# Bidirectional retention on one Trainium2 core: value and gate projections by seven block products in heads 1 to 7, the output summed in DRAM, gate and output weights placed anew

## The chip, the core and the metric

The kernel runs on one core of a Trainium2 chip, as one program written with a tile framework that places buffers, sets semaphores and orders the instructions of each engine. The engines are TensorE (PE, matrix products; PEld is its loading of weights), VectorE (DVE), ScalarE (ACT), GpSimd (POOL) and SyncE (SP, which here only issues loads). The metric is the device time of one execution in microseconds (us).

## The reference, cut to what matters

Two layers over 512 latent tokens and 256 context tokens of width 1024, all in float32. Layer 1 mixes tokens by retention; the change is in this mixer alone.

```python
q, k, v, g = jnp.split(h_lat @ w_in, splits, axis=-1)      # 8 heads: q, k 128 wide, v, g 256 wide
q = apply_rope(q); k = apply_rope(k * dk ** -0.5)
kc, vc = jnp.split(h_ctx @ w_in[:, ...], ...)              # context: k and v only
for d in range(2):                                         # forward and backward in time
    s_ctx = retention_final_state(kc, vc, log_decay[d])    # state carried in from the context
    o[d] = retention_chunked(q, k, v, log_decay[d], s_ctx) # decayed q.k scores times v, plus decayed q times state
on = group_norm_per_head(o[0] + o[1]) * gn_g
y_lat = (silu(g) * on) @ w_out                             # sum over the 8 heads
x = x + g1 * rmsnorm(y_lat)
```

## The kernel before, in words

Every product is made in three TensorE passes on float32 operands cut in two: `mm3` (L94 to L96) multiplies high by high, high by low and low by high. `split` makes the two halves: ACT copies the source to `hi` (L68), DVE subtracts to get `lo` (L69). A weight block is 128x1024 float32 (512 KB). `unit` loads it by SP (L54) into one of three "raw" buffers, and splits it into a weight slot. The slots go round; there are three (`w0` to `w2`) and in the retention three more (`phase("retp", 3)`). The raw buffers are shared with `ar`, the rows of the adaLN projection, a background job (`self.bg()`) that DVE sums (L214).

The order of instructions on each engine is fixed when the program is built, and each engine takes its list in order; semaphores make it wait for the others. In the retention, tiles of PSUM come from three pools of 4 (A), 2 (B) and 2 (C) banks.

Head 0 is written out for itself, among the work that ends layer 0. Each of the heads 1 to 7 does, in this order on PE:

- `rk`: the latent k projection (24 matmuls with 512 columns); meanwhile DVE does the end of the previous head's `norm`;
- `rt` and `rq`: `gated` transposes the previous head's gated output (8 transposes), and the q projection follows (24);
- `wr`: `out_group` multiplies the previous head's output by its two weight blocks `rwo`, and DVE adds each of the eight results into the sum `yr` in SBUF (L494);
- `kn`: transposes of k, decayed on ACT and DVE into `kd`;
- `rn` for v: three pairs of 128 tokens (context, latent, latent), each 48 matmuls with 256 columns, with the scores `rs` between them;
- `stc`, `stl`: `states` multiplies `kd` by v for the context and one latent chunk; a chain over ACT and DVE (`st`, `sc`, `cm`, `st`; L68, L1013, L1015, L69) makes the chunk states;
- `rn` for the gate: two pairs, 96 matmuls, each pair through SiLU on ACT (L1040);
- `ro` (`within`, chunk 0), two `rx` (`across`, from the states; DVE adds them into `of`, L1078), `rkc` (the next head's context k), `ro` (chunk 1), two `rx`, and `norm` (DVE L1094 to L1112 with a short piece on POOL, L1098 and L1101).

After head 7, `out_last` multiplies the outputs of heads 6 and 7 and passes the rows on to the second half of the layer.

Of the kernel before, what the change touches and what calls it, by code (L numbers as in the profile page):

```python
# [16 lines left out]
P = 128  # L17
D = 1024
# [22 lines left out]
class Trunk:  # L41
# [871 lines left out]
    def retention(self, y, final):  # L913
        S, V, T, G, a = self.S, self.V, self.T, self.G, self.a
        KS = float(np.float32(P) ** np.float32(-0.5))
        with ExitStack() as ctx:
            rp = self.phase(ctx, "retp", 3)
# [11 lines left out]
            qk = lambda h, o, n: self.unit(a["ret_qk"][(o + h) * P : (o + h + 1) * P], f"rw{n}{h}")  # L929
            vg = lambda h, o, n: [  # L930
                w8(self.unit(a["ret_vg"][(o + h * 2 + i) * P : (o + h * 2 + i + 1) * P], f"rw{n}{h}{i}"))
                for i in range(2)
            ]
# [92 lines left out]
            def nat(h, w, tp, dst):  # L1026
                ps = self.ps(f"rn{h}{tp}", "A", (P, 2, 256))
                for i in range(2):
                    hc = self.hcols(2 * tp + i)
                    for kk in range(KD):  # L1030
                        wk = w[kk // 4]
                        self.mm3(
                            ps[:, i, :], hc(kk), (wk[0][:, kk % 4, :], wk[1][:, kk % 4, :]), kk == 0, kk == KD - 1
                        )
                t = slice(2 * tp, 2 * tp + 2)
# [10 lines left out]
            def score(h, c):  # L1046
# [9 lines left out]
                s2 = d[c] = [rp.tile([P, 2, 256], F32R, name=f"sd{i}{h}{c}", tag=f"sd{i}", bufs=2) for i in range(2)]  # L1056
# [30 lines left out]
            def norm(h):  # L1087
# [14 lines left out]
                for t in range(4):  # L1102
                    on = rp.tile([P, 256], F32, name=f"on{h}{t}", tag="on", bufs=2)
# [11 lines left out]
            def gated(h):  # L1115
                d = hd[h]
                if h == 7:
                    gt = [x.rearrange("p (f c) -> p f c", f=2) for x in self.slot("gt7")]
                else:
                    gt = [rp.tile([P, 2, 512], F32R, name=f"gt{i}{h}", tag=f"gt{i}", bufs=1) for i in range(2)]  # L1120
# [16 lines left out]
            def w_out(h):  # L1137
                return [self.unit(a["ret_out"][(2 * h + f) * P : (2 * h + f + 1) * P], f"rwo{h}{f}") for f in range(2)]

            toks = (0, 1, 2, 3)  # L1140

            for h in range(8):
                vg_tiles(h)
                if h == 0:
                    wk = qk(h, 8, "k")
                    self.need(2)
                    k_ctx(h, wk)
                    wv = vg(h, 0, "v")
                    nat(h, wv, 2, "v")
                    self.need(0)  # L1150
                    wq = qk(h, 0, "q")
                    wg = vg(h, 16, "g")
# [3 lines left out]
                    for half in range(2):  # L1156
# [6 lines left out]
                        for n, f in enumerate(steps):  # L1163
# [6 lines left out]
                            if half and n == 2:  # L1170
                                k_nat(h)
                                score(h, 0)
                                score(h, 1)
                                states(h)
                    self.bg(4)
                else:
                    psk = self.ps(f"rk{h}", "A")
                    self.proj_t(psk, wk, 0)
                    k_lat(h, psk)
                    wq = qk(h, 0, "q")  # L1180
                    psq = self.ps(f"rq{h}", "A")
                    decay(h)
                    f = gated(h - 1)
                    self.proj_t(psq, wq, 0)
                    q_lat(h, psq)
                    self.bg()
                    if h < 7:
                        self.out_group(f, w_out(h - 1), y, toks, h == 1, None, f"r{h - 1}")
                    k_nat(h)
                    self.bg()  # L1190
                    wv = vg(h, 0, "v")
                    for tp in (2, 0, 1):
                        nat(h, wv, tp, "v")
                        if tp < 2:
                            score(h, tp)
                    self.bg()
                    wg = vg(h, 16, "g")
                    states(h)
                    for tp in range(2):
                        nat(h, wg, tp, "g")  # L1200
# [10 lines left out]
                if h < 7:  # L1211
                    k_ctx(h + 1, wk)
# [520 lines left out]
```

## Time and profile before

| | |
|---|---|
| median of 3 runs | 1902.22 us (1896.47 to 1906.23) |
| the profiled execution | 1893.99 us, of which the span from first to last instruction is 1892.2 us |
| mean granted TensorE clock in it | 0.983 |
| PE busy | 1800.1 us, 95% of the span, 10928 instructions |
| DVE, ACT, POOL busy | 1402.8, 1029.2 and 325.8 us |
| moved by DMA | 250.32 MB, mean 132 GB/s |

The clock is a share of full speed: 1.00 is full, 0.50 half. In the profile's lists of groups, a row names the line of the kernel, the engine, the operation, the tiles written and read, and behind the bar the busy time and the mean duration. "Idle" in brackets, or behind a second bar, is the time in which the engine stood still just ahead of the row, and the arrow names what it waited for. In a list by stretches (A:B, in us from the start) each row gives the length, then the busy time of PE, PEld, DVE, ACT and POOL with the instructions in brackets, the granted clock, the share of the DMA engines and GB/s. The answer for one tile gives its instructions with least, median and longest duration in ns, and the starts of the first and the last.

### The profile page before, as it was taken

What the parts mean: (1) busy time and instruction counts of PE and PEld (TensorE: products, weight loads), DVE (VectorE), ACT (ScalarE), POOL (GpSimd) and SP (SyncE); (2) the same over time, 40 slices, a digit from 0 to 9 for tenths busy, and PEclk for the clock granted to TensorE, in tenths of its full rate; (3) what the DMA queues carried; (4) which work ended last, traced back from release to release, by engine and by line L of the source; (5) the groups of instructions that cost most, each with busy time, mean ns of one, the idle gap of its engine ahead of it and who ended that gap; (6) DMA issues with size and microseconds to landing.
All of it is one profiled execution on the core that took longest, in us unless ns stands there. A gap on an engine that the chain in (4) does not pass through costs nothing. (4 is left out here: it accounts for less than half of the span.)

```text
span 1892.2 us, 28751 instructions
## 1 busy us (share of the span) xinstructions
PE 1800.1 (95%) x10928; PEld 1591.7 (84%) x10928; DVE 1402.8 (74%) x2352; ACT 1029.2 (54%) x1857; POOL 325.8 (17%) x446
## 2 busy tenths in 40 slices
PE   7998989979999999999989999999999989999998
PEld 4886867669889899998879889988989779889996
DVE  4844788679877778777877666675665689989877
ACT  6533545666555555555565434434444377666763
POOL 1102122130122222222121010011011100222221
PEclk9999999999999999999989999999999989999999
DMA  7333332132577877776744313322421225878772
GB/s 290 115 100 106 93 101 79 57 136 76 175 176 156 184 158 167 145 169 135 232 146 131 119 52 112 112 95 62 134 66 48 100 81 148 212 188 195 178 162 99
DMA packets 83823, 250.32 MB, mean 132 GB/s; under 512 B 10578, under 2 KB 12114, under 8 KB 83684
## 3 DMA queue, kind: packets, MB, share of 16 engines
q1 hardware_dynamic: 58436, 200.72, 32.8%
q0 software_dynamic: 25248, 47.75, 15.2%
q8 instruction: 86, 1.41, 0.3%
q14 instruction: 53, 0.43, 0.1%
HBM read 191.81 MB, written 39.85 MB: 122 GB/s over the span
## 5 line engine op out<-in xcount | busy, mean ns | idle before, releaser
L214 DVE SCALAR_TENSOR_TENSOR acc<-ar,cs,acc 128x512 f32<-128x512 f32 x256 | 189.5, 758 | 35.5 <-DMA ar<-in_adaw 19.7
L1463 POOL DMA_DIRECT2D yf<-yp x64 | 55.9, 873 | 260.2 <-ACT yp L1459 229.2
L1314 ACT ACTIVATE cv<-pre,cw 128x770 f32<-128x770 f32 (+1 forms) x88 | 80.9, 923 | 27.2 <-DVE pre L1307 25.9
L1315 DVE SCALAR_TENSOR_TENSOR cv<-pre,cw,cv 128x769 f32<-128x769 f32 (+1 forms) x88 | 77.2, 880 | 7.2 <-ACT cv L1314 7.2
L1459 ACT COPY yp<-wf 128x512 f32<-128x512 f32 x118 | 67.9, 577 | 18.1 <-PE wf L96 18.0
L1318 DVE SCALAR_TENSOR_TENSOR cv<-pre,cw,cv 128x769 f32<-128x769 f32 (+1 forms) x88 | 77.2, 881 | 0.7
L1302 ACT ACTIVATE pre<-px 128x256 f32<-128x256 f32 (+2 forms) x160 | 54.3, 367 | 41.8 <-PE px L93 33.6
L1098 POOL TENSOR_SCALAR rrr<-rmv 128x2 f32<-128x2 f32 x16 | 3.1, 193 | 363.2 <-DVE rmv L1095 363.2
L1463 POOL DMA_DIRECT2D yd<-ypg x48 | 42.1, 903 | 132.1 <-ACT ypg L1459 130.6
L1463 POOL DMA_DIRECT2D yd<-yp x48 | 42.6, 902 | 126.7 <-ACT yp L1459 126.6
L68 ACT ACTIVATE g<-cv 128x770 fp32r<-128x770 f32 (+1 forms) x44 | 32.5, 738 | 32.6 <-DVE cv L1322 32.4
L93 PE MATMUL px<-hs,wd 128*128 128x384 f32 x240 | 45.4, 337 | 0.0
L93 PEld LDWEIGHTS px<-hs,wd 128*128 128x128 f32 x240 | 42.3, 188 | 1.9 <-DVE pre L1307 0.4
L1307 DVE TENSOR_TENSOR pre<-pre,pz 128x256 f32<-128x256 f32 (+1 forms) x60 | 20.8, 371 | 29.2 <-PE pz L96 29.1
L69 DVE TENSOR_TENSOR g<-cv,g 128x770 fp32r<-128x770 f32 (+1 forms) x44 | 36.1, 821 | 7.4 <-ACT g L68 7.3
L1302 ACT ACTIVATE pre<-py 128x384 f32<-128x384 f32 (+1 forms) x40 | 17.5, 437 | 43.9 <-DVE cv L1318 25.6
L1322 DVE TENSOR_TENSOR cv<-cv 128x770 f32<-128x770 f32 (+1 forms) x44 | 36.2, 822 | 4.3 <-ACT cv L1321 3.1
L1321 ACT ACTIVATE cv<-cv 128x770 f32<-128x770 f32 (+1 forms) x44 | 32.7, 742 | 11.7 <-DVE cv L1318 11.6
L1078 DVE SCALAR_TENSOR_TENSOR of<-rx,e,of 128x256 f32<-128x256 f32 x64 | 28.9, 477 | 8.4 <-PE rx L96 7.9
L869 ACT ACTIVATE sc<-sc,sst 128x512 f32<-128x512 f32 x32 | 23.0, 719 | 22.1 <-DVE sc L860 21.6
L1459 ACT COPY ypg<-wf 128x512 f32<-128x512 f32 x54 | 30.7, 578 | 6.5 <-PE wf L96 6.4
L205 POOL MEMSET acc<- 128x512 f32 x32 | 19.1, 600 | 84.5 <-DVE al L69 62.2
(2985 smaller groups left out, 7181.1 us busy)
## 6 DMA issues: line engine op xcount, KB each, us to landing
ar<-in_adaw SPq DMA_DIRECT2D x96, 512.0 KB
yf<-yp POOLq DMA_DIRECT2D x64, 256.0 KB, 4.2
yd<-yp POOLq DMA_DIRECT2D x54, 256.0 KB, 5.2
yd<-ypg POOLq DMA_DIRECT2D x54, 256.0 KB, 5.0
fin<-xd SPq DMA_DIRECT2D x10, 512.0 KB
xd<-xd SPq DMA_DIRECT2D x8, 512.0 KB
xn<-in_x SPq DMA_DIRECT2D x6, 512.0 KB
xb<-in_x SPq DMA_DIRECT2D x6, 512.0 KB
```

What stands on the lines that cost most here:

```text
L68: self.S.activation(hi, src, AF.Copy)
L69: self.V.tensor_tensor(out=lo, in0=src, in1=hi.bitcast(F32), op=ALU.subtract)
L93: mm = lambda *p, **k: self.nc.tensor.matmul(*p, skip_group_check=True, **k)
L214: V.scalar_tensor_tensor(out=acc[s], in0=raw[:, kk * 512 : kk * 512 + 512], scalar=self.cs[:, 8 * s + k : 8 * s + k + 1], in1=acc[s], op0= ...
L1302: S.activation(pre[:, i, c : c + w], ps[:, b : b + w], AF.Copy, scale=scale)
L1314: S.activation(d, s, AF.Identity, scale=w1, bias=b)
L1315: V.scalar_tensor_tensor(out=d[:, 1:W], in0=s[:, 0 : W - 1], scalar=w0, in1=d[:, 1:W], op0=ALU.mult, op1=ALU.add)
L1318: V.scalar_tensor_tensor(out=d[:, 0 : W - 1], in0=s[:, 1:W], scalar=w2, in1=d[:, 0 : W - 1], op0=ALU.mult, op1=ALU.add)
L1321: S.activation(cv[:, 0], cv[:, 0], AF.Silu)
L1322: V.tensor_tensor(out=cv[:, 0], in0=cv[:, 0], in1=cv[:, 1], op=ALU.mult)
L1459: S.copy(v, ps)
L1463: G.dma_start((yd[t] if first else y[t])[:, o], v, accum_op=ALU.add)
```

## The change

**Products.** For heads 1 to 7 v and the gate of the latent tokens are taken together as one product, [512 tokens x 1024] by [1024 x (256 of v, 256 of the gate)]. Cut in two by two blocks ([256 x 512] by [512 x 256]) it was eight block products; now it is seven (the Winograd form of Strassen's scheme), with sums of the blocks on both sides.

```diff
+            def products(h):
...
+                X = bank("x")
+                product(X, blk[0, 0], u["b11"])
+                c11 = self.t2k(f"c11{h}", shape=(P, 2, 256))
+                S.copy(c11, X)
+                nat(h, [u["b11"], None], 2, "v", range(0, 4))
+                yield
+                Y = bank("y")
+                product(Y, blk["s", 1], u["t1"])
...
+                product(X, blk["s", 2], u["t2"], True)
...
+                product(Z, blk[0, 1], u["b21"])
+                V.tensor_tensor(out=c11, in0=c11, in1=Z, op=ALU.add)
...
+                nat(h, [None, u["b21"]], 2, "v", range(4, 8))
+                yield
+                product(X, blk["s", 3], u["t3"], True)
...
+                product(Y, blk["s", 4], u["b22"], True)
+                V.tensor_tensor(out=g[:, lo], in0=g[:, lo], in1=Y, op=ALU.add)
+                S.activation(g[:, lo], g[:, lo], AF.Silu)
+                yield
+                product(X, blk[1, 1], u["t4"], True)
+                self.split(v[0][:, hi], v[1][:, hi], X)
```

Each `product` is 24 matmuls with 256 columns (`rx`, `ry` and `rz` with the head's number are its banks). The sums of token blocks `s1` to `s4` are made once, in head 0, by `h_sums` (8 additions on POOL, 8 on DVE, 8 splits); the sums of weight blocks `t1` to `t4` in each head by `vg_units` on DVE and POOL.

**Output.** `y` is kept in DRAM tiles `yd`. Each of the eight results of a head is copied by ACT into one half of a two-part buffer `ypr` and added into DRAM by a DMA that POOL issues; the eight pieces stand between the products. Head 7 loads the sum back.

```diff
+                    v = part()
+                    S.copy(v, ps)
+                    if h == 0:
+                        G.dma_start(yd[t][:, o], v)
+                    else:
+                        G.dma_start(yd[t][:, o], v, accum_op=ALU.add)
```

**Buffers.** The retention has three weight slots in place of six; the output weights of heads 0 to 6 (`uwh`, `uwl` in the order) go into two pairs of their own, still through the raw buffers. The scores' halves `sd` have one buffer, the norm writes in place, the adaLN gate tiles are elsewhere.

**Order.** `within` of chunk 0 stands ahead of the last two products, and `states` behind them all and behind the next head's context k; the four `across` come together.

```diff
-                    wg = vg(h, 16, "g")
-                    states(h)
-                    for tp in range(2):
-                        nat(h, wg, tp, "g")
...
+                if h < 7:
+                    k_ctx(h + 1, wk)
+                states(h)
                 across(h, 0)
                 across(h, 1)
-                if h < 7:
-                    k_ctx(h + 1, wk)
                 within(h, 1)
```

Three places show what moves. All are at the end of head 3.

The loads on SP before the change (`rwk4`, `rwq4`, `rwv4`: k, q and v weights of head 4; `rwo3`: output weights of head 3, needed in head 4; `ar`: adaLN rows; the names behind "waits" are semaphores, those with HW count loads landed):

```order
L54 DMA rwk4r<-in_ret_qk 128x1024 [waits DMAHW2_49,DVE_49,Activation_49]
L54 DMA rwq4r<-in_ret_qk 128x1024 [waits DMAHW3_49,DVE_49]
L54 DMA ar_11901<-in_adaw 128x1024 [waits DMAHW4_49,DVE_49]
L54 DMA rwo30r<-in_ret_out 128x1024 [waits DMAHW5_49,DVE_49]
L54 DMA rwo31r<-in_ret_out 128x1024 [waits DMAHW6_49,DMAHW1_49,DVE_49]
L54 DMA ar_11999<-in_adaw 128x1024 [waits DMAHW0_49,DVE_49]
L54 DMA rwv40r<-in_ret_vg 128x1024 [waits DMAHW1_49,DVE_49]
```

and with it:

```order
L54 DMA rwk4r<-in_ret_qk 128x1024 [waits DMAHW6_49,DVE_49]
L54 DMA rwq4r<-in_ret_qk 128x1024 [waits DMAHW7_49,DVE_49]
L54 DMA rwv04r<-in_ret_vg 128x1024 [waits DVE_49]
L54 DMA ar_11971<-in_adaw 128x1024 [waits DMAHW3_49,DMAHW0_49,DVE_49]
L54 DMA rwo30r<-in_ret_out 128x1024 [waits DMAHW1_49,DVE_49]
L54 DMA rwo31r<-in_ret_out 128x1024 [waits DMAHW5_49,DMAHW4_49,DVE_49]
L54 DMA rwg14r<-in_ret_vg 128x1024 [waits DMAHW5_49,DVE_49]
```

The first v block of the next head now stands ahead of both output blocks, and `rwo30`, `rwo31` and `rwg14` each wait for the buffer of the one ahead: `rwo30` for that of `rwq4`, `rwo31` for that of `rwo30` (DMAHW4, the landing for which ACT waits below), `rwg14` for that of `rwo31` (DMAHW5).

ACT between the output weights and the last split of the states, before:

```order
L68 ACTIVATE rwo31h<-rwo31r 128x1024 [waits DMAHW1_49]
L68 ACTIVATE sd_11503<-sd_11494 128x512 [waits DVE_49]
L68 ACTIVATE st_11549<-stc_11523 128x2x256 [waits PE_49,Activation_49]
L1013 COPY sc_11554<-stc_11523 128x512 [waits DVE_49]
L68 ACTIVATE st_11549<-cm_11551 128x512 [waits DVE_49]
L1040 ACT_TABLE_LOAD
L1040 ACTIVATE rg_11093<-rn_11560 128x512 [waits PE_49]
L68 ACTIVATE rwv40h<-rwv40r 128x1024 [waits DMAHW3_49,PE_49]
L1040 ACTIVATE rg_11093<-rn_11610 128x512 [waits PE_49]
```

and with the change (`uwh` is an output weight's high half, `rv<-rx` v's last quadrant, `rg` the gate):

```order
L68 ACTIVATE rwq4h<-rwq4r 128x1024 [waits DMAHW1_49,PE_49]
L1308 ACTIVATE rg_11148<-rg_11148 128x512 [waits DVE_49]
L68 ACTIVATE rv_11146<-rx_11345 128x512 [waits PE_49]
L68 ACTIVATE rwb114h<-rwv04r 128x1024 [waits DMAHW2_49,Activation_49]
L68 ACTIVATE uwh_11985<-rwo30r 128x1024 [waits DMAHW4_49]
L962 ACTIVATE kc_11739<-rkc_11714 128x256 [waits PE_49]
L68 ACTIVATE st_11767<-stc_11741 128x2x256 [waits PE_49]
L1011 COPY sc_11772<-stc_11741 128x512 [waits DVE_49]
L1078 COPY of_11627<-ro_11790 128x512 [waits PE_49]
L68 ACTIVATE uwh_11991<-rwo31r 128x1024 [waits DMAHW5_49]
L68 ACTIVATE st_11767<-cm_11769 128x512 [waits DVE_49]
```

The split of the second output block now stands directly ahead of the last split of the states, where before both output blocks were split ahead of the first one. `rwq4h` now waits for PE: its slot is that of block `b22`, read by the last product but one.

PE at the `across`, before:

```order
L96 MATMUL ro_11671<-rv_11091,sd_11439 128x256
L94 MATMUL rx_11685<-st_11549,rq_11183 128x512
L95 MATMUL rx_11685<-st_11550,rq_11183 128x512
L96 MATMUL rx_11685<-st_11549,rq_11184 128x512
L94 MATMUL rx_11691<-st_11549,rq_11183 128x512
L95 MATMUL rx_11691<-st_11550,rq_11183 128x512
L96 MATMUL rx_11691<-st_11549,rq_11184 128x512
L94 MATMUL rkc_11697<-h0c,rwk4h 128x256
```

and with the change:

```order
L96 MATMUL ro_11790<-rv_11146,sd_11653 128x256
L94 MATMUL rx_11778<-st_11767,rq_11246 128x512
L94 MATMUL rx_11784<-st_11767,rq_11246 128x512
L94 MATMUL rx_11804<-st_11767,rq_11246 128x512
L94 MATMUL rx_11810<-st_11767,rq_11246 128x512
L94 MATMUL rk_11845<-h0c,rwk4h 128x512
L95 MATMUL rk_11845<-h1c,rwk4h 128x512
L95 MATMUL rx_11778<-st_11768,rq_11246 128x512
L96 MATMUL rx_11778<-st_11767,rq_11247 128x512
L95 MATMUL rx_11784<-st_11768,rq_11246 128x512
L96 MATMUL rx_11784<-st_11767,rq_11247 128x512
L95 MATMUL rx_11804<-st_11768,rq_11246 128x512
```

All four results for `norm` now come at once, directly ahead of the next head's `rk`, where `rkc` and a `ro` (36 matmuls) stood between the first two and the last two.

259 lines of the change are left out of this document (209 added, 50 removed).

## The prediction

> **What bounds the kernel now.** I read the page's busy shares first, then PE's waits, then the retention by stretches, from one head's `rk` to the next's.
>
> ```profile
> PE 1800.1 (95%) x10928; PEld 1591.7 (84%) x10928; DVE 1402.8 (74%) x2352; ACT 1029.2 (54%) x1857; POOL 325.8 (17%) x446
> ```
> ```profile
> PE rt L1124 <- DVE rg L1112: 2.9, 1, 2.9
> ...
> PE wrA L94 <- DVE of L1078: 1.5, 1, 1.5
> ```
> ```profile
> 1034.03:1104.99 70.96, 67.54 (x449) 61.02 (x448) 42.15 (x71) 32.71 (x48) 6.30 (x9) 0.98 0.30 96
> 1104.99:1171.29 66.30, 65.91 (x450) 60.00 (x449) 44.02 (x76) 26.66 (x39) 6.34 (x9) 1.00 0.31 100
> 1237.47:1303.89 66.42, 66.24 (x454) 60.07 (x452) 43.80 (x77) 27.34 (x40) 6.33 (x9) 1.00 0.31 96
> ```
>
> PE bounds it. These rows are heads 1, 2 and 4: a head takes 66.3 to 66.4 us and PE works 65.9 to 66.2 of them, at full clock. DVE has 22 us to spare in a head, ACT 39. So a matmul less is worth its full price, and any wait that the new order puts on PE costs in full too; here nothing on PE waits, except in head 1 (2.9 us) and at the end (1.5 us). The prediction is therefore a count of matmuls against a search for new waits.
>
> **Fewer matmuls: the gain.** Seven products instead of eight save 24 matmuls of 256 columns in each of 7 heads. Their spacing, from the gate projection (32 rows, 31 spacings):
>
> ```profile
> 1151.65 0.28 PE L94 MATMUL rn<-rwg20h,h0c 128*128 128x256 f32 x1
> ...
> 1155.30 0.28 PE L95 MATMUL rn<-rwg20l,h0c 128*128 128x256 f32 x1
> ```
>
> 3.65/31 = 0.1177 us; 24 of them 2.83 us; seven heads **-19.8 us**. The transposes, scores, `rk` and `rq` stay.
>
> **The states and the output weights (wait A).** Before, 96 gate matmuls (96 x 0.1177 = 11.3 us) stood between `stl` and `ro` and covered the chain that makes the states. Now only 12 matmuls of `ro` stand there (1.4 us). The order of ACT shows what is ahead of the last split `st<-cm`: the copy `of<-ro`, which waits for that `ro`, and in heads 1 to 4, behind that copy, the split of the second output block.
>
> ```profile
> 1154.89 0.63 ACT L68 ACTIVATE st<-cm 128x512 fp32r<-128x512 f32 x1 [0.94 <-DVE cm L1015]
> ...
> 1164.52 0.59 ACT L1070 COPY of<-ro 128x512 f32<-128x512 f32 x1 [0.77 <-PE ro L96]
> ```
>
> Without the output block PE waits from the end of `ro` for 0.59 + 0.63 and about 0.2 of hand-over (an estimate): 1.45 us. So it is in heads 5 to 7, where that split stands ahead of the states or is not there: 3 x 1.45 = **+4.4 us**.
>
> In heads 1 to 4 the loads decide. `rwq`, `rwo0` and `rwo1` go through one raw buffer one after the other, and `rwq`'s slot comes free only when product `b22` ends. The prices:
>
> ```profile
> L54 SPq DMA_DIRECT2D rwv41r<-in_ret_vg x1: 328/328/328, 1230.3 to 1230.3; - x1
> L68 ACT ACTIVATE rwv41h<-rwv41r x1: 1062/1062/1062, 1234.0 to 1234.0; 128x1024 fp32r<-128x1024 f32 x1
> L69 DVE TENSOR_TENSOR rwv41l<-rwv41r,rwv41h x1: 1226/1226/1226, 1235.1 to 1235.1; 128x1024 fp32r<-128x1024 f32 x1
> ```
> ```profile
> L69 DVE TENSOR_TENSOR rwk3l<-rwk3r,rwk3h x1: 1226/1226/1226, 1141.8 to 1141.8; 128x1024 fp32r<-128x1024 f32 x1
> ```
> ```profile
> L54 SPq DMA_DIRECT2D rwo20r<-in_ret_out x1: 328/328/328, 1143.0 to 1143.0; - x1
> L68 ACT ACTIVATE rwo20h<-rwo20r x1: 1045/1045/1045, 1147.4 to 1147.4; 128x1024 fp32r<-128x1024 f32 x1
> ```
>
> A load of 512 KB is 3.7 us from issue to ACT when ACT stands waiting for it (1230.3 to 1234.0), a split 1.06 + 1.23 = 2.3, and the next load is issued the moment DVE is done with the buffer (1141.8 + 1.2 = 1143.0). With 0 at the end of `b22`: `rwq` split at 2.3, `rwo0` landed at 6.0, split at 8.3, `rwo1` landed at 12.0, its high half at 13.1, `st<-cm` at 13.7. PE has meanwhile `t4`, `rkc`, `stc` and `stl`, `ro`: 84 x 0.1177 = 9.9 us. It waits 3.8 us, in four heads **+15.2 us**. Bounds: since `of<-ro` also stands ahead of the split, a load that lands in time still leaves 0.59 + 1.06 + 0.63 = 2.3 us; the slower load above (4.4, with others on the way) twice gives 5.2. I take 3.7, the row of the load that ACT waits for.
>
> **The norm (wait B).** All four `rx` now end together, and DVE's adds, statistics, POOL's root and the scaling run as one chain ahead of `rt`. The second pair of head 3 shows half of it:
>
> ```profile
> 1236.26 0.73 DVE L1104 TENSOR_SCALAR on<-of,rmv,rrr 128x256 f32<-128x256 f32 x2
> 1236.91 0.76 DVE L1112 TENSOR_TENSOR rg<-on,rg 128x256 f32<-128x256 f32 x2
> 1237.58 1.39 DVE L1078 SCALAR_TENSOR_TENSOR of<-rx,e,of 128x256 f32<-128x256 f32 x3
> 1238.88 0.42 DVE L1094 BATCH_NORM_STATS2 rbs<-of 128x6 f32<-128x256 f32 x1
> ...
> 1239.60 0.17 DVE L1095 BATCH_NORM_AGGREGATE rmv<-rbs 128x2 f32<-128x6 f32 x1
> ...
> 1243.00 0.74 DVE L1112 TENSOR_TENSOR rg<-on,rg 128x256 f32<-128x256 f32 x2
> ```
> ```profile
> L96 PE MATMUL rk<-h0c,rwk3l x8: 393/396/397, 1171.7 to 1176.6; 128*128 128x512 f32 x8
> ```
>
> It takes 1237.58 to 1243.74, 6.2 us, and `rk` (24 x 4.9/21 = 24 x 0.233 = 5.6 us) just covers it. Another pair adds four adds (4 x 0.46), two statistics and aggregates (1.0), two scalings and two products (0.7 each): 10.4 us. The cover is the six `rx` still to come and 22 of `rk` (28 x 0.233 = 6.5 us), and the four `rq` and three pairs of transposes ahead of the last ones (1.7): 8.2. `rt` waits 2.1 us at the starts of heads 2 to 7. Bounds: 0, if DVE starts the statistics between the adds as it did before, and 3.9, if the last two transposes have none of the 1.7 as cover.
>
> **The clock.** Two waits of PE in this profile, 2.92 us here and 2.7 at the end of the retention, are followed by a stretch at a lower granted clock:
>
> ```profile
> 1042.92 1.10 PE L1124 MATMUL rt<-ident,rg 128*128 128x128 f32 x6 [2.92 <-DVE rg L1112]
> ```
> ```profile
> 1044.09:1047.51 3.42, 3.42 (x10) 2.65 (x9) 2.70 (x4) 1.43 (x3) 0.00 (x0) 0.50 0.00 0
> ```
> ```profile
> PE ht L407 <- DVE yr L336: 2.7, 1, 2.7
> ```
> ```profile
> 1510.78:1514.20 3.42, 3.42 (x13) 2.90 (x14) 2.29 (x4) 1.92 (x6) 1.36 (x2) 0.64 0.49 151
> ```
>
> 3.42 us at half clock do 1.7 us less work. After wait A (3.8 us) that falls on `rx` and `rk`, and makes wait B shorter by as much, save for the part on `rx` (0.4 us, an estimate). So B is 2.5 in the four heads behind an A, 2.1 in the other two: **+14.2 us**.
>
> The Trainium skill ("TensorE: Matmul & The Clock Gate", sections "What's actually happening" and "HAM oscillation") puts the limit at a gap of about 3.4 us, in a window that runs freely. By that a wait of 3.8 us would seldom hold a whole window and the sum would be 1.6 us lower; the two rows above, with shorter gaps, disagree, and I go by them.
>
> **The end of the retention.**
>
> ```profile
> 1486.06 0.39 PE L96 MATMUL rx<-st,rq 128*128 128x512 f32 x1
> 1487.95 0.47 PE L94 MATMUL wrA<-rwo60h,gt 128*128 128x512 f32 x1 [1.50 <-DVE of L1078]
> ...
> 1494.71 0.40 PE L94 MATMUL wrB<-rwo70h,gt7h 128*128 128x512 f32 x1
> ```
> ```profile
> 1491.79 0.76 DVE L1112 TENSOR_TENSOR rg<-on,rg 128x256 f32<-128x256 f32 x2
> 1492.46 1.28 DVE L494 TENSOR_TENSOR yr<-wrA,yr 128x512 f32<-128x512 f32 x2
> ```
>
> From the last `rx` (1486.45) to `wrB` 8.3 us. With four `rx` at once the norm ends 10.4 - 1.4 = 9.0 us after the last, then transposes and gate as now (1492.55 to 1494.71, 2.2) and 0.9 of `yr` adds between: 12.1. **+3.9 us**, from 0 (the 24 `wrA` cover it) to 6.
>
> **Head 0.** `h_sums` puts 16 operations of 128x512 on DVE (0.60 apart) in the queue with the states and the norm, up to 9.6 us; against it stand head 1's wait (2.9) and its half clock (1.7), which can go. I take half of the first: 4.8 - 4.6 = +0.2, say **+0.5**; ends -4.6 and +9.6.
>
> **Costed at nothing.** The sums and splits of seven weight blocks for four add some 4 us to DVE and 10 to ACT in a head, within the 22 and 39 to spare. The copies of `y` replace the adds on DVE. A part of `ypr` is busy for a copy (0.6), an issue and a landing:
>
> ```profile
> L1463 POOL DMA_DIRECT2D yd<-yp x48 | 42.6, 902 | 126.7 <-ACT yp L1459 126.6
> ```
> ```profile
> yd<-yp POOLq DMA_DIRECT2D x54, 256.0 KB, 5.2
> ```
>
> 0.6 + 0.9 + 5.2 = 6.7 us; with two parts a piece may come each 3.4 us, and one comes per product and its `wr` (30 matmuls, over 4 us). If that cover fails, ACT waits in its copy, with the weight splits behind it.
>
> **Sum.** -19.8 + 4.4 + 15.2 + 14.2 + 3.9 + 0.5 = +18.4 us on the profiled 1893.99: 1912.4. The median of the runs, 1902.22, lies 8.2 us above that execution, so I give **1920 us** (1902.2 + 18.4 = 1920.6).
>
> **Rivals.** Under 0.5% (9.5 us) this kernel's runs cannot tell a change from none.
>
> - *The norm stays hidden* (not slower). If DVE works through the pairs as PE delivers them, so that the chain ends within the 8.2 us, B falls away and the clock with it, if A stays below 2.7 us or so: -19.8 + 4.4 + 4 x 3.8 + 3.9 + 0.5 = +4.2, 1906 us. For it: every DVE step here is far shorter than a PE stage. Against: the order of DVE has all eight adds ahead of the first statistics. It decides at a chain of 8.2 us in place of 10.4.
> - *Both joins short.* Loads that land in time and a hidden norm leave the 1.4 to 2.3 us of the states: -19.8 + 7 x 1.4 + 3.9 + 0.5 = -5.6, 1897 us; with these covered too 1884. Against it stands the order of ACT, where `of<-ro` waits for PE itself.
> - *The clock pays at every wait.* Half clock behind each A that B does not swallow, behind the states of heads 5 to 7 and at the end: 4 x 1.3 + 3 x 1.7 = +10.3 more, 1931 us. For it the 2.7 us row; against it waits of 2.1 and less have no such stretch here (`wrA`'s 1.5).
> - *The parts of `ypr` hold up ACT.* From a landing of about 8 us (twice 4 us and more per piece) each piece waits; at 2 us in one piece of each head +14, 1934 us. The 5.2 us row is against it.
>
> **Chances.** Forecast 0.56 (alone 1911 to 1930; 0.06 of it within 0.5%), norm hidden 0.16, both short 0.16 (0.12 of it below 1893), clock 0.08, `ypr` 0.04. Faster 0.12, within 0.5% 0.26, slower 0.62. The range leaves out the lowest 0.12 and most of the last two cases: 1892 to 1930.
>
> **What would show it.** 24 matmuls fewer in each head and a head of 63.5 us plus its waits; `rx` waiting for ACT's `st` 3.8 us at the ends of heads 1 to 4 with the split of `rwo1` just ahead of it, 1.4 in 5 to 7; `rt` waiting for DVE's `rg` some 2 us; half clock behind the first. I am wrong if `rwo1` is split well ahead of `stl`, if `rt` finds `rg` ready, or if a wait stands at the products.

## The result, and the profile after

The changed kernel takes **1960.09 us** (median of 4 runs, 1958.1 to 1963.77) against 1901.03 of the kernel before (4 runs): ratio 1.031, 95% interval 1.028 to 1.035. It is slower, as forecast, but by 59 us where 18 were expected, and lies 30 us above the range.

The profiled execution took 1963.77 us. The page's busy shares:

```profile
PE 1811.5 (92%) x10760; PEld 1590.7 (81%) x10760; DVE 1471.6 (75%) x2405; ACT 1079.0 (55%) x1954; POOL 402.9 (21%) x519
```

PE has 168 fewer matmuls (7 x 24) and yet 11 us more of busy time: at half clock a matmul with 256 columns counts as busy for 0.41 us, at full clock for 0.28. Here is the retention by stretches. Of the kernel before, these are the ones not shown yet (heads 0, 6 and 7, and the end):

```profile
970.59:1034.03 63.44, 61.49 (x487) 60.46 (x487) 47.68 (x77) 38.69 (x67) 10.93 (x12) 0.95 0.45 143
...
1370.15:1435.76 65.61, 65.61 (x454) 59.71 (x453) 38.12 (x68) 27.42 (x40) 6.96 (x10) 1.00 0.21 65
1435.76:1487.95 52.19, 50.69 (x376) 47.64 (x374) 28.62 (x54) 22.36 (x33) 5.79 (x8) 1.00 0.18 55
1487.95:1554.08 66.13, 55.24 (x328) 48.27 (x329) 53.32 (x94) 38.25 (x83) 11.18 (x18) 0.90 0.28 94
sum 583.49, PE 564.83 PEld 517.22 DVE 385.43 ACT 268.22 POOL 66.51; mean PE 62.76 PEld 57.47 DVE 42.83 ACT 29.80 POOL 7.39
```

And after the change, heads 0, 1, 2, 4, 6 and 7, the end, and the sum of the same nine stretches:

```profile
977.43:1051.55 74.12, 63.65 (x487) 61.29 (x488) 61.98 (x93) 42.38 (x74) 25.06 (x20) 0.91 0.38 117
1051.55:1119.92 68.37, 62.92 (x417) 56.75 (x416) 45.37 (x67) 36.92 (x56) 13.91 (x19) 0.99 0.41 132
1119.92:1195.87 75.95, 65.75 (x425) 58.39 (x424) 48.62 (x78) 34.52 (x53) 17.71 (x21) 0.95 0.48 119
...
1272.27:1348.49 76.22, 66.58 (x430) 59.05 (x428) 50.75 (x78) 34.80 (x54) 16.45 (x19) 0.95 0.45 111
...
1425.60:1494.27 68.67, 64.34 (x429) 57.60 (x428) 43.06 (x68) 33.48 (x52) 16.47 (x19) 1.00 0.38 78
1494.27:1556.76 62.49, 53.89 (x351) 48.98 (x350) 46.27 (x74) 28.25 (x42) 8.79 (x9) 0.92 0.34 113
1556.76:1626.60 69.84, 56.94 (x329) 49.32 (x330) 54.16 (x98) 38.35 (x83) 12.78 (x20) 0.88 0.27 90
sum 649.17, PE 570.42 PEld 511.71 DVE 453.28 ACT 318.29 POOL 144.26; mean PE 63.38 PEld 56.86 DVE 50.36 ACT 35.37 POOL 16.03
```

The retention with its end grew by 65.7 us in these two executions (their totals differ by 70, the medians by 59; 7 us of the difference arise in layer 0, whose order on PE is the same). Some ten of it are in head 0, as many in each of heads 2 to 5 and 7, three in head 6 and 3.7 at the end; head 1 became 2.6 shorter. PE's waits (in total, how many, the longest):

```profile
PE rx L94 <- ACT st L68: 35.4, 7, 7.8
PE rt L1133 <- DVE rg L1120: 14.6, 15, 1.6
...
PE rs L94 <- ACT rq L68: 3.9, 1, 3.9
...
PE kn L983 <- DVE m1k L954: 2.2, 1, 2.2
```

Both forecast waits are there, at the places named. `rt` waits as long as forecast; `rx` waits almost twice as long, and in heads 2 to 4 over 7 us each:

```profile
1194.00 2.08 PE L94 MATMUL rx<-st,rq 128*128 128x512 f32 x4 [7.77 <-ACT st L68]
...
1491.39 1.20 PE L94 MATMUL rx<-st,rq 128*128 128x512 f32 x4 [2.07 <-ACT st L68]
```

The order of ACT ahead of the first of these (head 2), in time:

```profile
1175.78 1.06 ACT L68 ACTIVATE rwk3h<-rwk3r 128x1024 fp32r<-128x1024 f32 x1 [7.69 <-DMA rwk3r<-in_ret_qk]
...
1180.16 1.06 ACT L68 ACTIVATE rwq3h<-rwq3r 128x1024 fp32r<-128x1024 f32 x1
...
1186.50 1.06 ACT L68 ACTIVATE uwh<-rwo20r 128x1024 fp32r<-128x1024 f32 x1 [2.81 <-DMA rwo20r<-in_ret_out]
...
1192.37 1.06 ACT L68 ACTIVATE uwh<-rwo21r 128x1024 fp32r<-128x1024 f32 x1 [1.85 <-DMA rwo21r<-in_ret_out]
1193.33 0.61 ACT L68 ACTIVATE st<-cm 128x512 fp32r<-128x512 f32 x1
```

From the start of the split of `rwq3` to the end of `st<-cm` it is 13.8 us, against 13.7 in the forecast (14.2 and 14.4 in heads 3 and 4): the two loads and splits are sized right. But ACT stood 7.69 us ahead of them, for the k weights of the next head, and came to `rwq3` 4.0 us after product `b22` had ended (the next one, `t4`, begins at 1176.15). That was not in the forecast. In heads 3 and 4 ACT was 3.2 and 2.8 us late in the same way, behind waits of 7.2 and 6.8 us for the k weights. Stretches at half clock in heads 1 to 7, two of the seven and the sum of all:

```profile
1189.62:1199.86 10.24, 5.86 (x14) 4.62 (x15) 4.37 (x9) 3.76 (x5) 0.00 (x0) 0.50 0.29 102
...
1503.65:1507.06 3.41, 3.41 (x11) 2.74 (x11) 2.98 (x6) 1.78 (x3) 0.00 (x0) 0.50 0.00 0
...
sum 40.96, PE 30.01 PEld 25.01 DVE 19.52 ACT 15.26 POOL 0.00; mean PE 4.29 PEld 3.57 DVE 2.79 ACT 2.18 POOL 0.00
```

PE worked 30 us at half clock there: 15 us lost. The second row lies behind head 7's `rt`, 12 us after the `rx` that waited 2.07; that `rx` itself has no stretch behind it.

### The profile page after: what moved, and what is told of

It is laid out like the page before. It is cut to its first block, busy times and chain, and to the rows that moved or that the text cites. A ratio compares the mean times of both kernels' runs of the same rounds, so it can differ in the third digit from the quotient of the medians.

```text
span 1962.0 us, 28754 instructions
## 1 busy us (share of the span) xinstructions
PE 1811.5 (92%) x10760; PEld 1590.7 (81%) x10760; DVE 1471.6 (75%) x2405; ACT 1079.0 (55%) x1954; POOL 402.9 (21%) x519
## 3 DMA queue, kind: packets, MB, share of 16 engines
q8 instruction: 84, 1.38, 0.3%
## 5 line engine op out<-in xcount | busy, mean ns | idle before, releaser
L1177 POOL DMA_DIRECT2D yr<-ypr x40 | 34.8, 870 | 137.1 <-ACT ypr L1173 136.0
L94 PE MATMUL rx<-st,rq 128*128 128x512 f32 x32 | 13.9, 557 | 35.4 <-ACT st L68 35.4
L1527 ACT ACTIVATE cv<-cv 128x770 f32<-128x770 f32 (+1 forms) x44 | 32.7, 742 | 11.4 <-DVE cv L1524 11.3
L94 PE MATMUL wr<-uwh,gt 128*128 128x512 f32 x96 | 38.6, 402 | 0.0
L94 PEld LDWEIGHTS rx<-st,rq 128*128 128x128 f32 x32 | 7.5, 258 | 37.9 <-ACT st L68 36.8
```

The lines of the kernel that those rows point to most:

```text
L94: mm(out, lhs[0], rhs[0], start=first, stop=False)
L1177: G.dma_start(yd[t][:, o], v, accum_op=ALU.add)
```

## The experiments

A wait at `rx` is called A and one at `rt` B, as in the prediction. A kernel that ran four times has a ratio to the kernel before (1898 to 1903 us); one that ran once has a time alone. Diffs are cut, and are against the changed kernel, but for the first.

**The order alone, in the kernel before** (`e7_before_order`).

```diff
-                    states(h)
                     for tp in range(2):
...
                 within(h, 0)
+                if h < 7:
+                    k_ctx(h + 1, wk)
+                if h > 0:
+                    states(h)
+                within(h, 1)
                 across(h, 0)
                 across(h, 1)
-                if h < 7:
-                    k_ctx(h + 1, wk)
-                within(h, 1)
```

> The kernel before with one part of the change: states behind the gate and the next head's context k, and the four across together; no block products, no y in DRAM, six weight slots. Theory (the order costs what it uncovers, the rest of the loss is loads): rx waits about 2 us (the end of the states' chain) and rt about 2 us in each of heads 1 to 7, with a half clock for one or the other; 5 to 6 us a head, 1935 to 1945 us. Rival (six slots keep ACT ahead, nothing is late): 1901 to 1910 us.

1940.68 us, ratio 1.022 (1.018 to 1.026). Its waits:

```profile
PE rx L94 <- ACT st L68: 15.1, 7, 2.2
PE rt L1124 <- DVE rg L1112: 12.8, 17, 1.7
```

With eight products, `yr` in SBUF and six slots, moving the states and the `across` alone costs 42 us, as expected: A is 2.1 to 2.2 in every head, B up to 2.4, and five stretches of 3.4 us at half clock follow them. Some 3 of the 42 are not A or B: head 0 is that much longer, with a wait of 2.7 us for the table `dist` and one more such stretch. What is left is the larger part of the 59.

**No adaLN rows in heads 1 to 6** (`e2_no_ada`; they come in head 7, so the total says nothing).

```diff
                 q_lat(h, psq)
-                self.bg()
...
-                    if n in (1, 3, 5):
-                        self.bg()
```

> The changed kernel with the adaLN rows taken out of heads 1 to 6; all that is left of them is done in head 7, so the time as a whole is not to be compared, only heads 2 to 5. Theory (raw buffers): without the four rows in a head the k weights land in time, ACT is not behind, and rx waits 1.5 to 2.5 us; a head takes 68 to 70 us in place of 76. First rival (transfers of y): rx still waits about 7 us. Second rival (order alone): the same 7 us.

Head 2 as a stretch, and A:

```profile
1113.80:1184.79 70.99, 66.52 (x424) 59.37 (x423) 45.75 (x71) 34.28 (x52) 15.70 (x17) 0.95 0.40 89
```
```profile
PE rx L94 <- ACT st L68: 12.4, 6, 2.1
```

A is 2.07 in all six heads, where head 2 had 7.8. The k weights of head 3 are now issued 16.6 us ahead of their split (1145.5 and 1162.0), so it takes the rows in the shared raw buffers to make them late. But the list of ACT changed as well: here both output blocks are split ahead of the states' first split in heads 1 to 5, so 2.07 is the wait with no output block in the chain. How much of the 7.8 is the late k weights and how much the output block, this run alone does not tell; the next one does.

**The k weights out of the raw buffers** (`e16_wk_own`, heads 2 to 7, through the buffer of the first gate block).

```diff
+                raw = rp.tile([P, 1024], F32, name=f"rwk{h}r", tag="vgr", bufs=1)
+                self.load(raw, src)
+                x = self.slot(f"rwk{h}")
+                self.split(*x, raw)
```

> The changed kernel with one load placed elsewhere: the k weights of heads 2 to 7 come through the buffer of the first gate block instead of a raw buffer. Theory (in heads 2 to 4 the k weights land late, ACT stands at their split with rwq and all else queued behind it, and that lateness is what the forecast's 3.8 us lacked): ACT no longer waits 7 us for them, rwq is split right after product b22, and rx waits 3.4 to 4.5 us in heads 2 to 4 in place of 7.1 to 7.8; 1940 to 1948 us. Rival (any load on the way is as late, with the transfers of y): rx waits 6 us or more, above 1952 us.

1941.64 us in a single run. The tile of head 3's k weights, and A:

```profile
L54 SPq DMA_DIRECT2D rwk3r<-in_ret_qk x1: 328/328/328, 1150.8 to 1150.8; - x1
L68 ACT ACTIVATE rwk3h<-rwk3r x1: 1062/1062/1062, 1162.2 to 1162.2; 128x1024 fp32r<-128x1024 f32 x1
```
```profile
PE rx L94 <- ACT st L68: 23.1, 7, 4.8
```

The load is issued 11.4 us ahead of its split, ACT no longer waits for it, and A in heads 1 to 5 is 3.5, 4.8, 4.4, 3.7 and 2.5 in place of 4.4, 7.8, 7.3, 7.1 and 4.6. ACT's list still has the second output block directly ahead of the last split of the states in heads 1 to 4, and there the forecast's 3.8 fits (4.1 on average). Moving that one load takes back 12.3 of the 15.8 us by which A was too small. It also leaves the raw buffers one load less for all others; that part is not told apart.

**The output weights out of the raw buffers, loaded a head earlier** (`e1_wo_own`, through the same buffer).

```diff
+                for f in range(2):
+                    raw = rp.tile([P, 1024], F32, name=f"rwo{h}{f}r", tag="vgr", bufs=1)
+                    self.load(raw, src(f))
```

> The changed kernel with one thing different: the output weights of heads 0 to 6 are loaded through the buffer that the first gate block uses (free in the second half of a head) and are asked for a head earlier, so they no longer stand in the row of the three raw buffers, and both are split ahead of the states. PE's order is the same. Theory (the raw buffers, shared by k, q, v, gate, output weights and the adaLN rows, are the cause): rx waits some 1.5 us at the ends of heads 1 to 5 in place of 4.4 to 7.8, the half clock behind it goes, 1930 to 1940 us. First rival (the eight transfers of y to DRAM in each head slow the loads): the waits stay above 4 us, 1950 to 1960 us. Second rival (the place of states and across alone makes the wait): no change, 1960 us.

1956.04 us, 1.028 (1.025 to 1.031). A fell from 4.4 to 2.07 in head 1, but only to 5.6 or 5.7 in heads 2 to 4, and in head 5 it rose from 4.6 to 5.1 (28.1 in all), so the theory that the output blocks make A failed in the larger part. ACT still stands 7.4 us for head 3's k weights, at the end of head 2:

```profile
1171.88 1.06 ACT L68 ACTIVATE rwk3h<-rwk3r 128x1024 fp32r<-128x1024 f32 x1 [7.44 <-DMA rwk3r<-in_ret_qk]
```

**The accumulating transfers** (`e3_no_accum` leaves them out, `e9_plain_write` makes plain writes of them).

The diff is that of `e9`, after which `y` holds only the last part written.

```diff
-                        G.dma_start(yd[t][:, o], v, accum_op=ALU.add)
+                        G.dma_start(yd[t][:, o], v)
```

> The changed kernel without the seven accumulating transfers of y to DRAM in heads 2 to 7 (the sum is left at head 0's part); the copies by ACT stay. Theory (raw buffers): rx waits as before, 7 us at the ends of heads 2 to 4, time within 6 us of 1960. First rival (transfers of y): the loads get faster, rx waits 3.8 us or less, 1935 to 1945 us.

> The changed kernel with the transfers of y as plain writes in place of accumulating ones (only the last head's part is then in y). Theory (each transfer, as such, stands in the way of the loads): half of the gain or less of leaving them out: rx waits 5 to 7 us in heads 2 to 4. Rival (it is the reading and adding in DRAM): rx waits 3.4 to 4 us, as without the transfers.

1942.63 and 1944.75 us (single runs). A of both, and the DMA row of `y` (KB each, median us to landing) after and with plain writes:

```profile
PE rx L94 <- ACT st L68: 21.6, 7, 4.4
```
```profile
PE rx L94 <- ACT st L68: 22.9, 7, 4.9
```
```profile
yr<-ypr POOLq DMA_DIRECT2D x48, 256.0 KB, 4.4
```
```profile
yr<-ypr POOLq DMA_DIRECT2D x48, 256.0 KB, 2.6
```

Leaving the transfers out and making them plain gives nearly the same A, so it is the reading and adding in DRAM that counts, not the bytes written. The load of `rwk3` takes 5.5 us from issue to ACT in the changed kernel (first row; ACT starts at 1175.78) and 3.6 without the transfers:

```profile
L54 SPq DMA_DIRECT2D rwk3r<-in_ret_qk x1: 328/328/328, 1170.3 to 1170.3; - x1
```
```profile
L54 SPq DMA_DIRECT2D rwk3r<-in_ret_qk x1: 327/327/327, 1163.1 to 1163.1; - x1
L68 ACT ACTIVATE rwk3h<-rwk3r x1: 1060/1060/1060, 1166.6 to 1166.6; 128x1024 fp32r<-128x1024 f32 x1
```

So the 7 us need both the rows and weights in one set of buffers and the slow transfers: without either A is 2 to 5. ACT, which takes its list in order, passes the lateness on to the states.

**The sums of token blocks** (`e10_no_sums` leaves them out).

```diff
+                for n, b in ((1, (1, 0)), (2, (1, 1)), (3, (0, 0)), (4, (0, 1))):
+                    blk["s", n] = A[b]
+                if blk:
+                    return
```

> The changed kernel without the sums of token blocks (the products use four plain blocks in their place, so v and the gate are not the reference's). Theory (the sums stand on DVE and GpSimd ahead of head 0's rope, and their cost is head 0's): head 0 takes 64 to 66 us in place of 74, the heads behind it are unchanged, 1948 to 1952 us. Rival (head 0 is longer because its loads and splits moved): 70 us or more.

1945.07 us (single run); head 0 is back at

```profile
972.89:1036.96 64.07, 60.49 (x486) 59.00 (x487) 47.55 (x74) 39.60 (x68) 11.31 (x12) 0.97 0.42 138
```

and the other heads are as after (A 4.2, 7.7, 6.7, 6.6, 4.7). The sums cost 10 us, all in head 0 (the rest of the 15 between the two times is spread over layer 0 and the other heads, and is not explained). How, the changed kernel's POOL, DVE and PE show there (`swk` and `m1k` belong to the rope of k):

```profile
1015.93 4.72 POOL L1205 TENSOR_TENSOR hsgt<-h0c,h1c 128x512 f32<-128x512 f32 x2 [3.76 <-ACT rg L1048]
1020.62 1.28 POOL L1205 TENSOR_TENSOR hsvgr<-h0c,h1c 128x512 f32<-128x512 f32 x1
1021.87 1.72 POOL L953 TENSOR_TENSOR swk<-swk,sin 128x512 f32<-128x512 f32 x1
```
```profile
1020.69 1.77 DVE L1212 TENSOR_TENSOR hsgt<-hsgt 128x512 f32<-128x512 f32 x1 [2.43 <-POOL hsgt L1205]
...
1029.98 0.68 DVE L1212 TENSOR_TENSOR hsgt<-hsvgr,hsgt 128x512 f32<-128x512 f32 x1
```
```profile
1025.33 0.44 PE L983 MATMUL kn<-ident,m1k 128*128 128x128 f32 x2 [2.25 <-DVE m1k L954]
1030.17 0.58 PE L94 MATMUL rs<-rq,rk 128*128 128x256 f32 x1 [3.89 <-ACT rq L68]
```

POOL adds token blocks until 1021.87 and only then turns to the rope, DVE stands for POOL and then splits sums between the rope's steps, and PE waits for k, then for q; 10.2 us at half clock come with it.

**Moving the sums** (`e6_combo_hold`: all of them behind head 0's states, on top of `e5_combo` below; `e17_hold_half`: half, on top of `e14_spread_wk` below, with the adaLN rows of heads 4 to 6 loaded by SP). The diff is that of `e17`.

```diff
+                    if m == 1:
+                        s1 = hd[0]["st"][1].bitcast(F32)[:, 0, 0:1]
+                        for x in (r21, r22, r11, r12):
+                            G.tensor_tensor(out=x[:, 0, 0:1], in0=s1, in1=s1, op=ALU.add)
```

> The same three things, and the sums of token blocks in head 0 held back until its states are made (four small additions on GpSimd that read the states and write into the buffer of the sums). Theory: head 0 goes from 74 back to 64 to 66 us (its waits for rope's results on DVE and its half clock go), so 8 to 10 us below the kernel without the hold. Rival (head 0 is longer for another reason, such as DVE and GpSimd slowing each other): the sums cost the same in a later place, and less than 3 us are won.

> This is the kernel of e14_spread_wk with the second half of the token sums in head 0 (eight of the sixteen operations of h_sums and their splits) held until head 0's second state is there, and the adaLN rows of heads 4 to 6 loaded by SP again. Theory (the sums ahead of the rope and the states are what makes head 0 ten us longer, and half of them can stand behind the states without harm): head 0 goes from 72.9 us to 68 or less, head 1 grows by at most 2, the other heads stay at 65 to 70, and the time falls from 1922 to 1910 to 1916. Rival (the sums cost DVE and POOL time wherever they stand before head 1's products, so that what head 0 gains head 1 pays, as when all of them were held): heads 0 and 1 together stay at 143 to 144 us and the time stays at 1919 to 1925. In both the kernel before, at 1902, stays faster.

`e6`: 1940.54 us, 1.022 (1.019 to 1.026), against 1930.81 without the hold: head 0 falls to 66.6 us but head 1 rises from 66.7 to 82.7. `e17`: 1923.45, 1.013 (1.009 to 1.017), no better than `e14`; the waits for the rope in head 0 (6.3 us in `e14`) are down to 0.5, yet head 0 stays at 73.7, with 2.2 us of other waits behind the rope, and this ahead of it:

```profile
997.08 0.55 PE L94 MATMUL rq<-h0c,us4h 128*128 128x256 f32 x1 [3.11 <-DMA dist<-in_dist]
```

Both times the time did not fall, as the rivals had it. A third run that held half the sums, `e13` below, differs: without adaLN rows in head 0 it takes 70.1 us there, against 73.1 in `e11`, and its head 1 is not longer for it (71.1 against 72.2). Whether half the sums could be hidden without that wait for a table, which came with half clock behind it and which `e7` shows too (2.7), is open.

**Other orders of the last products.** In `e4_b22_last` the product `b22` comes between the states and `ro`, with `t4` ahead of it; `e5_combo` adds `e1`'s buffer and puts `rkc` back between two pairs of `across`; `e8_pieces_late` moves output pieces and `within` there as well. The diff is that of `e5`; `e4` has only the line with `next`, behind `states`.

```diff
+                states(h)
+                next(p, None)
+                within(h, 1)
+                across(h, 0)
+                across(h, 1)
                 if h < 7:
                     k_ctx(h + 1, wk)
-                states(h)
-                across(h, 0)
-                across(h, 1)
-                within(h, 1)
                 across(h, 2)
```

> The changed kernel with the last two products swapped and the gate's last product (24 matmuls, 2.8 us) put between the states and ro; the split of the second output block then stands behind the last split of the states. Theory (raw buffers): the wait is what ACT has left to do when the loads land; 2.8 us more cover and one load less ahead of it, so rx waits 0 to 2 us in heads 1 to 5, 1930 to 1940 us. Second rival (order alone): about the same, 2.8 us less in each head, 1935 to 1940. First rival: 4 us stay, 1945.

> Three things together on the changed kernel: output weights out of the raw buffers, the gate's last product between the states and ro, and the four across two and two with the next head's context k between them. Theory (the waits of rx are loads that come late, slowed by the transfers of y; the wait of rt is the norm in one piece): rx waits under 1 us in all heads and rt under 0.5, with no half clock in heads 1 to 6; a head takes 64 to 66 us in place of 76, 1905 to 1920 us. Rival (the transfers of y hold up the loads whatever the order): rx still waits 2 to 4 us in heads 2 to 5, 1935 to 1945 us.

> The version with output weights out of the raw buffers and the gate's last product behind the states, now with two more covers: two of the eight output pieces (12 matmuls, 2.8 us) stand between v's last product and the states, ro of both chunks ahead of rx, and the next head's context k between the two pairs of across. Theory (each wait is the chain ahead of it less the matmuls beside it): stl no longer waits (2.0 and 1.0 us in the version without the pieces there), rx and rt wait under 0.7 us, a head takes 65 to 66 us in heads 2 to 5 in place of 71 to 72, 1900 to 1912 us. Rival (the loads are late whatever stands beside them, from the transfers of y): the waits move to rkc or to the products, a head stays at 70 us or more, 1925 to 1935 us.

`e4`: 1946.77 us, 1.024 (1.021 to 1.027); A is down to 10.8 us in all and B up to 21.7; the split of an output weight (1.20 us on DVE) now stands inside the norm's chain. `e5`: 1930.81, 1.017 (1.014 to 1.020): B is 6.5 and A 5.1, and a new wait stands at the states, for the split of v's last quadrant:

```profile
PE stl L94 <- ACT rv L68: 8.6, 4, 2.4
```

`e8`: 1961.08, 1.030 (1.026 to 1.034), nothing gained: A is 19.6, and products wait 16.6 us for DVE's gate sum. In head 3 DVE had stood 3.8 us for an adaLN row ahead of that sum, and ACT 4.4 us for an output block ahead of A. None of the three came to the time expected of it.

**q ahead of the transposes** (`rq` ahead of `rt`, k's transposes behind the first product; `e11_order_rows` also loads the adaLN rows through the buffer of the first gate block, `e12_order_only` doesn't, `e13_rows_later` also takes the rows out of head 0 and holds half the sums).

```diff
                 decay(h)
+                self.proj_t(psq, wq, 0)
+                q_lat(h, psq)
                 f = gated(h - 1)
```

> The changed kernel with two things. The order: v's last product ahead of the gate's last one, which stands between the states and ro; the q projection ahead of the transposes of the gated output; the first product and the context half of v ahead of the k transposes. The buffers: in heads 1 to 7 the adaLN rows are loaded through the buffer of the first gate block, free in the second half of a head, and not through the three raw buffers; output weights stay in the raw buffers. Theory (the adaLN rows in the raw buffers hold DVE and make the k weights late, the transfers of y only lengthen each load; the norm in one piece makes rt wait): rx and rt wait under 1 us, a head takes 64 to 67 us in heads 2 to 5, 1905 to 1918 us. Rival (the transfers of y are enough to make the loads late): rx or the products still wait 3 us or more in a head, 1925 us or more.

> The same order, with the adaLN rows in the raw buffers as in the changed kernel. Theory (rows in the raw buffers): the loads are late again, 2 to 4 us of waits at rx or at the products in heads 1 to 5 that the version with moved rows doesn't have, 10 to 20 us above it. Rival (order alone): within 5 us of it.

> The version with order and moved rows, and head 0 relieved: no adaLN rows in head 0 (five steps of them in a later head in place of four), and the second half of the sums of token blocks held until head 0's states are made. Theory (head 0's 10 us are DVE's queue: sums, and sums waiting for GpSimd, ahead of rope): head 0 takes 66 to 69 us in place of 73, the other heads as in the version without, 1897 to 1912 us. Rival (the sums cost the same wherever they stand): head 1 is longer by what head 0 gains.

`e11`: 1953.16 us, 1.028 (1.026 to 1.030). `e12`: 1936.37 (single run). `e13`: 1935.86, 1.019 (1.017 to 1.022). B is gone from the heads in all three (2.0 us are left, at the end), and the wait goes elsewhere. `e12`:

```profile
PE rs L94 <- ACT ypr L1173: 27.6, 11, 5.3
```

Two output pieces stood side by side, and the scores wait for the copy that frees the bank of the second. In the longest of these waits that copy is queued on ACT behind a k weight for which ACT stood 8.1 us; six of the eleven are 1.99 us, at an earlier pair of pieces. One buffer for four rows (`e11`) makes it worse by 17 us, where 10 to 20 us less were expected: DVE then waits for the rows one at a time.

**The best order found** (`e14_spread_wk`: that order, the k weights out of the raw buffers as in `e16`, one output piece behind each product).

```diff
+                    if n == 2:
+                        score(h, 0)
+                    if n == 7:
+                        score(h, 1)
                     o()
...
+                    if n in (2, 4, 6, 7):
                         self.bg()
...
+                within(h, 0)
```

> The order of the earlier version (v's last product ahead of the gate's, that one between states and ro, q ahead of the transposes), the k weights in the buffer of the first gate block, and the eight output pieces one by one between single products, none back to back. Theory (with k weights in time and the y buffer never asked twice in a row, ACT keeps up): scores, rx and rt wait under 1 us each, a head takes 64 to 67 us in heads 2 to 5, 1900 to 1915 us; what remains over the kernel before is head 0's 10 us and the end. Rival (DVE standing at late adaLN rows is enough by itself): waits of 3 us or more at the products or the scores, 1925 us or more.

1921.86 us, 1.011 (1.008 to 1.014), between the 1900 to 1915 expected and the rival's 1925. Head 6, and the longest waits that remain in heads 1 to 5:

```profile
1394.52:1459.60 65.08, 63.84 (x430) 57.75 (x428) 42.19 (x69) 33.54 (x53) 16.85 (x19) 1.00 0.39 82
```
```profile
PE rx L93 <- DVE rg L1313: 12.0, 5, 4.2
```

But for the end of the retention (2.3 us in all), the states and the norm no longer hold PE up; a product waits 1 to 4 us for its bank behind DVE's gate sum, and another 0.9 in heads 1 to 6 behind `kd`. With head 0 at 72.9 and the end 4 us longer it is still slower than before, and no version ran faster than the kernel before.

## Why the prediction was right or wrong

The direction and both waits were right. The terms, against the profiled execution (65.7 us in the nine stretches):

| term | forecast | measured | from |
|---|---|---|---|
| seven products, net of what waits cost beyond their listing | -19.8 | -9 to -12 | below |
| A, heads 1 to 7 | +19.6 | +35.4 | PE's waits |
| B, heads 2 to 7 | +12.6 | +11.9 | 14.6 less head 1's (0.8) and the end's (1.9) |
| half clock in heads 1 to 7 | +1.6 (6.8 less 5.2 that B was to take back) | +15.0 | half of 30.01 |
| head 0, and what goes in head 1 | +0.5 | +6.9 | 10.7, less 2.1 of head 1's wait and its 1.7 |
| head 7's q and weights | 0 | +2.7 | 1.38 + 1.27 |
| the end | +3.9 | +3.7 | 69.84 - 66.13 |
| sum | +18.4 | +64 to +67 | |

- **A** is the first step that failed: "`rwq` split at 2.3" from the end of `b22`. It took for granted that ACT is free at that moment. In head 2 it was 4.0 us late, having stood for `rwk3`, and in heads 3 and 4 it was 3.2 and 2.8 us late; `e16` moves that load and gets 3.5 to 4.8 in heads 1 to 4. The step behind it, 13.7 us for two loads and splits in turn, measured 13.8 to 14.4. Without an output block in the chain A was put at 1.45; it is 2.07 or 2.13 in heads 6 and 7, and 2.07 everywhere in `e2`. Head 5's 4.6 was to be such a head and was not: there too ACT stood 7.4 us for the k weights.
- **The clock** is the second. The forecast had one stretch of 3.42 us behind each of four long A, 1.7 us lost in each (6.8), and let B take back 1.3 of each (5.2). Neither held. The half clock sets in 3.4 to 5.1 us into the waits of 7 us and lasts 3.4 to 5.9 us beyond them; the five stretches behind A cost 10.3 us. Two more in head 7, behind its B and its late q, cost 4.7. And B took almost nothing back: behind such a stretch it is 2.2, 1.5, 2.2, 2.2 and 1.9 us, without one (head 7) 2.1. So B's size came out as worked out (11.9 against 12.6) only because that step failed; why B does not shrink is open.
- The rival on the clock ("pays at every wait", 0.08) was nearer, but is not right either. A wait of 2.07 can be enough; in `e2` a stretch at 0.50 begins with the end of such a wait:

```profile
1109.35 2.06 PE L94 MATMUL rx<-st,rq 128*128 128x512 f32 x4 [2.07 <-ACT st L68]
```
```profile
1109.40:1112.82 3.42, 3.42 (x8) 2.75 (x9) 1.11 (x2) 1.20 (x1) 0.00 (x0) 0.50 0.00 0
```

  Yet the 2.07 and 2.13 of heads 6 and 7 in the changed kernel have none. Of the thirty waits of 2.0 to 2.3 us at `rx` in ten traces (this kernel, `e1` to `e4`, `e7`, `e9` to `e11`, `e16`), sixteen have a stretch at half clock that begins within 1.5 us of their end, and fourteen have not. The reason given against the rival, that 1.5 us at `wrA` trips nothing, was true and left 2.07 undecided.
- **Head 0**: the bound of +9.6 was worked out and then halved, and as much came (10.7), but by another way, so the likeness is luck. The bound counted DVE's operations in the queue with the states and the norm; it is POOL's adds and DVE's splits ahead of the rope, and the half clock behind the waits, that count (`e10`, 10 us).
- **The gain** was too large, by less than it seems. Head 6 without its listed waits (4.33 us) is 64.34 at full clock, 1.3 below the 65.61 before; `e14`'s is 63.84, 1.8 below; 2.83 were expected. Counted from start to start in the two traces, head 6 has 240 matmuls of v and the gate in 28.2 us before and 216 in 25.8 after: 2.4 us saved. The other 1.1 us lie in the other groups, most of it where they wait. There the trace counts idle time from a matmul's end, 0.28 us after its start, where the next would have begun after 0.118, so a wait costs some 0.16 us more than is listed (an estimate).
- **Head 7**, not priced: with no output pieces between its products, it runs ahead of its weights, and of q:

```profile
1518.66 0.38 PE L95 MATMUL rs<-rq,rk 128*128 128x256 f32 x1 [1.38 <-DVE rq L69]
1521.50 0.58 PE L93 MATMUL rn72v<-rwb217h,h0c 128*128 128x256 f32 x1 [1.27 <-ACT rwb217h L68]
```

- **The end** is right in size, in part by luck: from the last `rx` to `wrB` it is 11.2 us, where 12.1 were worked out and 8.3 stood before; another 1.0 us comes behind that, where a stretch at half clock is 13.65 us long in place of 10.24. **The cover of `ypr`** held; its copies hold PE up in an order that puts two pieces together (`e12`). The rivals "norm hidden" and "both short" fell with A and B. (The second figure of the latter is mis-added: -19.8 + 3.9 + 0.5 gives 1887, not 1884.)

## What to carry to other kernels

Price a move on a full engine by what it uncovers: here the chain of two engines behind the states and the norm was hidden by 96 matmuls, and laying it bare cost some 39 us over the heads (`e7`, without head 0's 3), more than the saved product could give. Where an engine takes its list in order, ask of each load ahead of the critical step when it can be issued, not only how long it takes: one late block among shared buffers moved everything behind it by 3 to 4 us. On this clock a wait can cost more than its length: a wait of 2 us in every head is to be priced with 1.7 us of half clock behind about every second one, as it was in these traces.

## What the runs showed of the hardware

- A transfer of 256 KB that adds into DRAM took 4.4 us (median) to land, a plain write 2.6, and beside the former a load of 512 KB took 5.5 us to its use where it took 3.6 without.
- Stretches at half clock come in lengths of 3.41 us and its multiples (6.83, 10.24), and sixteen of thirty waits of 2.0 to 2.3 us have one behind them. The limit of about 3.4 us of idleness in the Trainium skill ("TensorE: Matmul & The Clock Gate", section "What's actually happening") is not what these rows show; the length of its window agrees with the 3.41.
- An addition of 128x512 on DVE that takes 0.68 us alone took 1.77 beside an addition on POOL, and two of POOL's in a row took 4.72 beside DVE's, where two others took 2.52; most of it is in the first (3.48). The Trainium skill ("SBUF — State Buffer", section "SBUF: two separate sides") describes a port pair that the two lock in turn; the rows agree in kind.
